# One block for a whole decoder-trunk kernel, with its instruction order from a detailed timing model

## The chip, the core and the metric

The kernel runs on one core of a Trainium2 chip. The core has five engines with an instruction queue each: TensorE (PE) for matmuls and transposes, VectorE (DVE), ScalarE (ACT), GpSimd (POOL) and SyncE (SP), which here issues the DMAs. Each engine takes its own instructions in the order in which the program holds them; engines wait for each other by semaphores. The metric is the time of one execution on the device in microseconds, as the median of several runs.

## What is computed

Two layers of a decoder trunk over 512 tokens of width 1024, in float32. Each layer adds three terms to h: a mixer of three kinds of attention heads, a gated feed-forward of width 2816, and a per-layer embedding.

```python
for i in range(DEPTH):                     # DEPTH = 2
    hn = rms_norm(h, norm_mix[i])
    proj = hn @ w_in[i]                    # split into q, k, v of all head groups, gates
    ...
    o_nsa = nsa_attention(...)             # 8 heads in 2 groups: compressed, selected, window keys
    o_fox = forgetting_attention(...)      # 4 heads, softmax with a learned decay
    o_sb = stick_breaking_attention(...)   # 4 heads
    o = rms_norm(jnp.concatenate([o_nsa, o_fox, o_sb], axis=2), head_norm)
    h = h + o.reshape(b, s, MIX_WIDTH) @ w_out[i]
    hn = rms_norm(h, norm_ffn[i])
    h = h + (jax.nn.silu(hn @ w_ffn_gate[i]) * (hn @ w_ffn_up[i])) @ w_ffn_down[i]
    gate = jax.nn.sigmoid(rms_norm(h, norm_ple[i]) @ w_ple_gate[i])
    h = h + (p[i] @ w_ple_proj[i]) * gate
return rms_norm(h, norm_final)
```

## The kernel before

**Arithmetic and tiles.** Every float32 operand of a large product is split into a high and a low part (`halves`, lines 197 to 201: ACT copies, DVE or POOL subtracts), and a product is three matmuls (`mm3`, lines 221 to 225: high by high, high by low, low by high). Tokens are four tiles of 128, the width is eight. Weights arrive in `wraw` (three buffers, by DMAs of SP) and leave as `whl` (five buffers). PSUM has eight banks in four groups: "d" (2), "s" (3), "t" (2), "o" (1).

**Stages.** `mixer` (line 456) normalizes h and transposes it (`norm_T`, line 372: tile `xnT` in PSUM, copied to `xT` by ACT, its low part by DVE at line 388), and runs the projections and four kinds of attention. `feed_forward` (line 1120) follows, then `layer_embedding` (line 1168), whose accumulators `ge` hold the embedding product and the gate product side by side; `pg` is the gate's sigmoid.

**The attention chains.** In `softmaxes` (line 773) an item takes scores on PE (`sc`, lines 787 and 789), a maximum on DVE (`mx`, line 792), exponentials on ACT (`p`, line 795), a reciprocal on DVE (`rc`), a scaling on POOL (line 800), transposes on PE (`pTp`, line 808), copies on ACT and DVE (`pT`, lines 813 and 814), and products with the values on PE (`no` for NSA, line 1004; `fo` for the forgetting heads, line 860). `cmp_maps` (line 917) opens each of the two NSA groups: compressed scores (`cs`, line 922), their copy (`cse`), transposes (`csT`, line 929), a softmax in `ce` on DVE and ACT (lines 934 to 949, its exponential at 939), and transposes back (`pcT`, line 952). A finished head goes through `head_out` and `norm_pair` (lines 606 to 641): `obot`, `pair`, `sq`, a matmul `ms`, two `rs`, `pair`, `on`. The tile `on` is what the output projection reads: partly in `accr` (streams W067, W167, W00123, W10123, woven into the attention), the last two k tiles with `wo4` and `wo5` in `acco` (lines 1107 to 1116), which also adds the result to h (`add_h`, line 1025).

**What sets the order.** Python traces the program in one sequence. `weave` (line 102) interleaves an attention stream with filler streams, as the string at line 1093 says:

```python
        spec = "KC;cmp:SQ,SK,SV;sb:NKS,NKW,GT,NQ0;nsa0:NQ1,FV,FQ;nsa1:FR,FK,W067;fox:W167,W00123,W10123;45"
```

The framework's scheduler then orders the instructions of each engine. It weighs their priority (the place in the trace, moved by `prio`, line 123, whose offsets OFE, OFN, OFP stand at line 100), the dependencies, the free buffers, and its own model of how long an operation takes. `tc.issue_after` adds a dependency by hand.

Of the kernel before, what the change touches and what calls it, by code (L numbers as in the profile page):

```python
# [42 lines left out]
def hybrid_trunk_kernel(  # L43
# [24 lines left out]
    upool = ctx.enter_context(tc.tile_pool(name="upool", bufs=1))  # L68
    small = ctx.enter_context(tc.tile_pool(name="small", bufs=6))
    ps = ctx.enter_context(tc.tile_pool(name="ps", bufs=1, space=PSUM))  # L70

    def bank(tag, shape=(P, 512), dt=F32, name=None):
        bufs = {"d": 2, "s": 3, "t": 2, "o": 1}[tag]
        return ps.tile(list(shape), dt, name=name or f"ps_{tag}", tag=tag, bufs=bufs)
# [1258 lines left out]
```

## Time and profile before

| | us |
|---|---|
| median of 3 runs | 1573.04 (1572.74 to 1576.78) |
| the profiled execution | 1575.22 |
| its span, first to last instruction | 1573.5 |
| PE busy in it | 1516.4 |
| DVE, ACT, POOL busy | 746.1, 733.1, 577.4 |
| mean granted clock of PE | 0.992 of full |

The profiled execution was one of the same program; what lies between its span and its time is start and end of the launch. A row of a timeline gives an instruction's start and its length in us, its engine, the line of the kernel, the operation and its tiles; in brackets stands how long the engine was idle before it, and what ended that. A row of a table of stretches gives the busy time of each engine in a part of the span, so that the idle time of an engine is the stretch less that. Matmuls overlap in the pipeline of PE: a row's length is longer than the distance to the next start. The clock column is the granted clock of PE, 1.00 being the higher of its two levels (2.4 GHz) and 0.50 the lower (1.2 GHz).

### The profile page before, as it was taken

Reading aid. Unit: us, or ns where it says so; the run is one execution under the profiler, and the core shown is the slowest. Engines: PE = TensorE matmul, PEld = TensorE weight load, DVE = VectorE, ACT = ScalarE, POOL = GpSimd, SP = SyncE. Lnnn points to the kernel's source line nnn. Section 1 sums busy time; section 2 is a strip of 40 time slices with the busy share of each in tenths; the row PEclk is TensorE's granted clock in tenths of the full one; section 3 lists DMA queues with packets and bytes.
Section 4 is the critical chain, followed back from the end, with each engine's and each line's share of the span. In section 5 each row is a group of like instructions: output and inputs, shape, how many; then the busy total and the mean of one; then the engine's idle time right before and its main releaser. Section 6 shows DMA issues by size and latency. Waiting matters only on the chain.

```text
span 1573.5 us, 23178 instructions
## 1 busy us (share of the span) xinstructions
PE 1516.4 (96%) x8626; PEld 1286.3 (82%) x8626; DVE 746.1 (47%) x1588; ACT 733.1 (47%) x1561; POOL 577.4 (37%) x636
## 2 busy tenths in 40 slices
PE   6999999999999999999999999999999999999997
PEld 6898877879888888888988988778788888888887
DVE  7777869763211111214386878796621111112153
ACT  5467667654333332323355767686433333323243
POOL 4323545453333333321233235465333333323223
PEclk9999999999999999999999999999999999999999
DMA  5411321122333323321224121212133323333221
GB/s 163 136 56 42 82 68 34 48 95 70 97 102 94 94 94 121 119 96 67 81 72 126 49 71 52 80 33 75 55 103 98 94 94 94 100 114 121 94 70 65
DMA packets 114449, 134.58 MB, mean 86 GB/s; under 512 B 6864, under 2 KB 91936, under 8 KB 114336
## 3 DMA queue, kind: packets, MB, share of 16 engines
q1 hardware_dynamic: 114336, 133.10, 27.5%
q8 instruction: 68, 1.11, 0.3%
q14 instruction: 45, 0.37, 0.1%
HBM read 122.59 MB, written 2.10 MB: 79 GB/s over the span
## 4 chain that ended last, share of the span: by engine, by line
PE 73%; DVE 9%; issue 7%; POOL 4%; ACT 4%; DMA 3%; SPq 0%; POOLq 0%; ACTq 0%; DVEq 0%
PE gu L223 10%; PE gu L224 10%; PE gu L222 10%; PE acc L222 6%; PE acc L223 6%; PE acc L224 6%; PE sc L787 2%; PE pTp L808 2%; PE no L1004 2%; PE accr L222 2%; POOL whl L201 2%; PE accr L223 2%; PE accr L224 2%; PE z L698 1%; DMA wraw<-in_w_ple_gate_dram 1%
## 5 line engine op out<-in xcount | busy, mean ns | idle before, releaser
L201 POOL TENSOR_TENSOR whl<-wraw,whl 128x512 fp32r<-128x512 f32 (+2 forms) x248 | 333.7, 1350 | 706.8 <-ACT whl L198 607.6
L198 ACT ACTIVATE whl<-wraw 128x512 fp32r<-128x512 f32 (+2 forms) x416 | 260.6, 631 | 483.0 <-PE gu L224 290.3
L201 DVE TENSOR_TENSOR whl<-wraw,whl 128x512 fp32r<-128x512 f32 x168 | 127.7, 761 | 496.8 <-ACT whl L198 496.1
L224 PE MATMUL gu<-xT,whl 128*128 128x512 f32 (+1 forms) x768 | 287.4, 374 | 0.0
L223 PE MATMUL gu<-xT,whl 128*128 128x512 f32 (+1 forms) x768 | 287.3, 374 | 0.0
L222 PE MATMUL gu<-xT,whl 128*128 128x512 f32 (+1 forms) x768 | 286.8, 373 | 0.0
L223 PEld LDWEIGHTS gu<-xT,whl 128*128 128x128 f32 x768 | 144.2, 188 | 27.5
L224 PEld LDWEIGHTS gu<-xT,whl 128*128 128x128 f32 x768 | 144.2, 188 | 27.4
L222 PEld LDWEIGHTS gu<-xT,whl 128*128 128x128 f32 x768 | 144.4, 188 | 27.1
L223 PE MATMUL acc<-whl,hid 128*128 128x512 f32 x352 | 139.7, 397 | 0.0
L222 PE MATMUL acc<-whl,hid 128*128 128x512 f32 x352 | 139.4, 396 | 0.0
L224 PE MATMUL acc<-whl,hid 128*128 128x512 f32 x352 | 138.8, 394 | 0.0
L800 POOL TENSOR_SCALAR p<-p,rc,gt 128x128 f32<-128x128 f32 (+3 forms) x128 | 79.2, 629 | 71.1 <-DVE rc L798 20.8
L795 ACT ACTIVATE p<-sc,mx 128x128 f32<-128x128 f32 (+3 forms) x160 | 83.9, 536 | 23.0 <-DVE mx L792 21.1
L814 DVE TENSOR_TENSOR pT<-pTp,pT 128x512 fp32r<-128x512 f32 (+2 forms) x120 | 70.6, 595 | 21.2 <-ACT pT L813 20.2
L813 ACT ACTIVATE pT<-pTp 128x512 fp32r<-128x512 f32 (+2 forms) x120 | 62.1, 527 | 38.6 <-PE pTp L808 37.3
L224 PEld LDWEIGHTS acc<-whl,hid 128*128 128x128 f32 x352 | 66.4, 189 | 15.3
L222 PEld LDWEIGHTS acc<-whl,hid 128*128 128x128 f32 x352 | 66.2, 188 | 15.1
L223 PEld LDWEIGHTS acc<-whl,hid 128*128 128x128 f32 x352 | 66.1, 188 | 15.3
L222 PE MATMUL acc<-whl,xT 128*128 128x256 f32 x256 | 74.0, 290 | 1.3 <-DVE rot_b L410 0.6
L792 DVE TENSOR_REDUCE mx<-sc 128x1 f32<-128x384 f32 (+4 forms) x120 | 70.2, 592 | 7.4 <-PE sc L789 7.2
L224 PE MATMUL acc<-whl,xT 128*128 128x256 f32 x256 | 73.3, 288 | 0.0
(298 smaller groups left out, 3320.7 us busy)
## 6 DMA issues: line engine op xcount, KB each, us to landing
wraw<-in_w_ffn_gate_dram SPq DMA_DIRECT2D x44, 512.0 KB, 3.6
wraw<-in_w_ffn_up_dram SPq DMA_DIRECT2D x44, 512.0 KB, 3.6
wraw<-in_w_ffn_down_dram SPq DMA_DIRECT2D x44, 512.0 KB, 3.6
wraw<-in_w_in_dram SPq DMA_DIRECT2D x36, 512.0 KB, 3.5
wraw<-in_w_out_dram SPq DMA_DIRECT2D x16, 512.0 KB, 3.7
wraw<-in_w_ple_gate_dram SPq DMA_DIRECT2D x16, 512.0 KB, 3.5
sw<-nq SPq DMA_DIRECT2D x32, 128.0 KB, 2.3
wraw<-in_w_in_dram SPq DMA_DIRECT2D x8, 280.0 KB, 2.9
```

Of the source, the lines that this page charges most:

```text
L198: se.activation(whl[:, 0], raw[:, lo:lo + n], AF.Copy)
L201: eng.tensor_tensor(whl[:, 1], raw[:, lo:lo + n], f(whl[:, 0]), op=ALU.subtract)
L222: i = te.matmul(acc, lhsT=lh, rhs=rh, start=start, stop=False, skip_group_check=True)
L223: te.matmul(acc, lhsT=lh, rhs=rl, start=False, stop=False, skip_group_check=True)
L224: te.matmul(acc, lhsT=ll, rhs=rh, start=False, stop=stop, skip_group_check=True)
L787: te.matmul(s[:, c:c + w], lhsT=lhsT, rhs=rhs, start=(j == 0), stop=False, skip_group_check=True)
L792: ve.tensor_reduce(mx, sv, axis=AX.X, op=ALU.max, negate=True)
L795: se.activation(e[:, u * n:(u + 1) * n], s[:, u * n:(u + 1) * n], AF.Exp, bias=mx[:, u:u + 1], accum_out=sm[:, u:u + 1])
L800: ge.tensor_scalar(e[:, u * n:(u + 1) * n], e[:, u * n:(u + 1) * n], rc[:, u:u + 1], gates[u] if gates else 1.0, op0=ALU.mult, op1=ALU.mult)
L808: te.transpose(pt[:, kt, :], e[:, kt * P:(kt + 1) * P], ident)
L813: se.activation(hi, src, AF.Copy)
L814: ve.tensor_tensor(lo, src, f(hi), op=ALU.subtract)
```

## The change

One line is added behind the pools. All that is traced after it, which is the whole computation, belongs to one block, and the order within this block is made with the scheduler's more detailed timing model. Nothing else is changed: the instructions of each engine, their operands, and the buffers are the same, and the numbers of lines and buffers rise by one.

```diff
--- before.py
+++ after.py
@@ -68,6 +68,7 @@
     upool = ctx.enter_context(tc.tile_pool(name="upool", bufs=1))
     small = ctx.enter_context(tc.tile_pool(name="small", bufs=6))
     ps = ctx.enter_context(tc.tile_pool(name="ps", bufs=1, space=PSUM))
+    ctx.enter_context(tc.block(schedule_with_timeline_sim=True))
 
     def bank(tag, shape=(P, 512), dt=F32, name=None):
         bufs = {"d": 2, "s": 3, "t": 2, "o": 1}[tag]
```

What moves is seen at three places. In the rows, buffers carry numbers where names alone would not tell them apart.

**ACT at the opening of the first NSA group, layer 0.** `cse` and `ce` belong to the compressed scores, `p` to the score sets of the group's first items (two heads by two branches of 128 columns make the first set, two branches of 256 each of the next two), `whl` to weights of the filler streams. Before:

```order
L926 ACTIVATE cse<-cs 128x512
L198 ACTIVATE whl<-wraw 128x520
L939 ACTIVATE ce<-ce 128x512
L795 ACTIVATE p,sm<-sc,mx 128x128 x4
L795 ACTIVATE p,sm<-sc,mx 128x256 x2
L198 ACTIVATE whl<-wraw 128x520
L795 ACTIVATE p,sm<-sc,mx 128x256 x2
L795 ACTIVATE p,sm<-sc,mx 128x384 x2
L954 ACTIVATE pc<-pcT 128x512
```

With the change:

```order
L927 ACTIVATE cse<-cs 128x512
L796 ACTIVATE p,sm<-sc,mx 128x128 x4
L796 ACTIVATE p,sm<-sc,mx 128x256 x4
L940 ACTIVATE ce<-ce 128x512
L796 ACTIVATE p,sm<-sc,mx 128x384 x3
L955 ACTIVATE pc<-pcT 128x512
```

The exponential of `ce` moved from ahead of the score sets to behind three of them, and the weight splits left the place. On PE, at the same place, 40 matmuls of the query projection stood between `csT` and `pcT`; now seven matmuls of another projection stand there, and more score matmuls.

**PE in the tail of the mixer, layer 0.** `pTp` and `fo` are those of the last forgetting head, `accr` with `on_2583` and `on_3415` is the output projection of earlier heads, `acco` the one of the last two k tiles. Before:

```order
L808 MATMUL pTp<-ident,p 128x128 x7
L860 MATMUL fo<-pT,fv 128x256 x4
L222 MATMUL accr<-whl,on_2583 128x512
L860 MATMUL fo<-pT,fv 128x256
L223 MATMUL accr<-whl,on_2583 128x512
L224 MATMUL accr<-whl,on_2583 128x512
L222 MATMUL accr<-whl,on_2583 128x512
L860 MATMUL fo<-pT,fv 128x256 x7
L223 MATMUL accr<-whl,on_2583 128x512
```

With the change (`on_4105` is the tile of the last two k tiles, `wo_4316` and `wo_4321` are `wo4` and `wo5`):

```order
L809 MATMUL pTp<-ident,p 128x128 x2
L861 MATMUL fo<-pT,fv 128x256 x7
L223 MATMUL acco<-wo_4316,on_4105 128x512
L224 MATMUL acco<-wo_4316,on_4105 128x512
L225 MATMUL acco<-wo_4316,on_4105 128x512
L809 MATMUL pTp<-ident,p 128x128 x7
L861 MATMUL fo<-pT,fv 128x256 x12
L635 MATMUL ms<-sq,ones_176 128x512
L223 MATMUL acco<-wo_4321,on_4105 128x512
L224 MATMUL acco<-wo_4321,on_4105 128x512
```

Before, two groups of twelve `accr` matmuls stood from the first `fo` of the last head to behind `ms`, and twelve `acco` with `wo4` behind them. With the change the `accr` and `acco` matmuls stand ahead of the seven `pTp`, and `fo`, `ms` and `acco` with `wo5` follow each other directly.

**PE in the per-layer embedding, layer 0.** `acc` is the end of the feed-forward, `ge` the embedding product, `xnT` the transposes of the normalized h. Before:

```order
L223 MATMUL acc_6592<-whl,hid 128x512
L380 MATMUL xnT<-ident,xn 128x128
L224 MATMUL acc_6592<-whl,hid 128x512
L380 MATMUL xnT<-ident,xn 128x128
L222 MATMUL acc_6592<-whl,hid 128x512
L380 MATMUL xnT<-ident,xn 128x128
```

With the change:

```order
L223 MATMUL ge<-we,pleT 128x256
L381 MATMUL xnT<-ident,xn 128x128 x4
L224 MATMUL ge<-we,pleT 128x256
L225 MATMUL ge<-we,pleT 128x256
L223 MATMUL ge<-we,pleT 128x256
```

Single transposes that alternated with single matmuls became four in a row, with several `ge` matmuls before the next four, and the feed-forward's last matmuls moved ahead of all of them.

## Rows read from the trace of the kernel before

**Rows 1.** The page, part 1: busy time of each engine, share, instructions.
```profile
PE 1516.4 (96%) x8626; PEld 1286.3 (82%) x8626; DVE 746.1 (47%) x1588; ACT 733.1 (47%) x1561; POOL 577.4 (37%) x636
```

**Rows 2.** Stretches of layer 0: window, length, busy per engine (instructions), PEclk, DMA.
```profile
156.00:183.00 27.00, 26.42 (x188) 22.49 (x188) 22.06 (x66) 17.20 (x47) 14.48 (x18) 1.00 0.38 99
227.00:250.00 23.00, 20.70 (x98) 15.49 (x97) 19.77 (x44) 12.73 (x36) 10.66 (x13) 0.93 0.15 46
250.00:290.00 40.00, 39.31 (x266) 32.47 (x265) 35.57 (x92) 31.80 (x81) 22.84 (x37) 1.00 0.16 41
328.00:346.00 18.00, 15.60 (x67) 12.13 (x66) 10.60 (x15) 6.65 (x12) 5.45 (x5) 0.91 0.33 103
346.00:365.00 19.00, 17.30 (x116) 14.91 (x116) 14.74 (x23) 9.77 (x24) 5.75 (x12) 1.00 0.01 3
715.00:740.00 25.00, 23.09 (x146) 19.58 (x145) 15.45 (x23) 11.28 (x22) 6.04 (x10) 1.00 0.24 84
765.00:802.00 37.00, 32.97 (x271) 31.89 (x270) 20.95 (x39) 15.12 (x36) 9.18 (x18) 1.00 0.20 58
```

**Rows 3.** The same columns for stretches of layer 1.
```profile
1104.00:1124.00 20.00, 18.22 (x84) 13.55 (x83) 12.58 (x17) 9.07 (x19) 9.01 (x10) 1.00 0.34 105
1490.00:1518.00 28.00, 26.12 (x172) 22.64 (x171) 16.29 (x25) 11.58 (x23) 6.02 (x10) 1.00 0.22 75
1518.00:1545.00 27.00, 25.27 (x212) 24.86 (x211) 13.26 (x18) 8.45 (x16) 12.63 (x8) 1.00 0.18 59
```

**Rows 4.** Waits of PE over the span: who for whom, us, times, longest.
```profile
PE sc L787 <- ACT p L795: 4.6, 2, 2.3
PE ge L222 <- DVE pg L1237: 3.4, 3, 1.6
PE cmp L523 <- DVE whl L201: 1.9, 2, 1.0
```

**Rows 5.** Timeline of PE at 327 us: start, length, engine, line, operation, tiles.
```profile
327.29 0.40 PE L222 MATMUL accr<-whl,on 128*128 128x512 f32 x1
327.52 0.39 PE L223 MATMUL accr<-whl,on 128*128 128x512 f32 x1
```

**Rows 6.** Timeline of PE and DVE, opening of the first NSA group.
```profile
159.52 0.66 PE L929 MATMUL csT<-ident,cse 128*128 128x128 f32 x4
...
168.39 0.60 PE L952 MATMUL pcT<-ident,ce 128*128 128x128 f32 x4
...
160.22 0.69 DVE L934 TENSOR_TENSOR ce<-csT,amask 128x512 f32<-128x512 f32 x1 [3.56 <-PE csT L929]
...
167.33 0.82 DVE L949 TENSOR_TENSOR ce<-ce,crc 128x512 f32<-128x512 f32 x1
```

**Rows 7.** The page, part 5: the score reductions of all softmaxes.
```profile
L792 DVE TENSOR_REDUCE mx<-sc 128x1 f32<-128x384 f32 (+4 forms) x120 | 70.2, 592 | 7.4 <-PE sc L789 7.2
```

**Rows 8.** Timelines of PE, DVE and ACT, layer 0's mixer tail.
```profile
330.48 1.12 PE L808 MATMUL pTp<-ident,p 128*128 128x128 f32 x4 [2.00 <-POOL p L800]
334.03 1.00 PE L860 MATMUL fo<-pT,fv 128*128 128x256 f32 x7
337.18 1.05 PE L634 MATMUL ms<-sq,ones 128*128 128x512 f32 x2
...
332.26 0.69 DVE L814 TENSOR_TENSOR pT<-pTp,pT 128x512 fp32r<-128x512 f32 x1 [1.65 <-ACT pT L813]
340.02 1.39 DVE L638 SCALAR_TENSOR_TENSOR pair<-pair,hgT,rs 128x512 f32<-128x512 f32 x1 [2.42 <-ACT rs L637]
...
341.44 0.63 ACT L640 ACTIVATE on<-pair 128x512 fp32r<-128x512 f32 x1 [0.42 <-DVE pair L638]
```

**Rows 9.** Stretches of 2 us behind three gaps of PE.
```profile
242.00:244.00 2.00, 2.00 (x6) 1.50 (x7) 2.00 (x11) 2.00 (x9) 0.80 (x2) 0.50 0.00 0
332.00:334.00 2.00, 2.00 (x8) 1.70 (x7) 0.69 (x1) 0.23 (x1) 0.00 (x0) 0.53 0.00 0
...
1020.00:1022.00 2.00, 1.65 (x9) 1.20 (x10) 2.00 (x9) 2.00 (x11) 0.38 (x1) 1.00 0.01 4
```

## The prediction

> **What bounds the kernel now.** I read the busy table first. TensorE (PE) is busy for 1516.4 of 1573.5 us, the other engines for less than half of the span each [rows 1]. So this is a PE-bound kernel, and a change that only reorders can do two things: take from, or add to, the 57.1 us in which PE stands idle. Next I cut the span into stages with the table of stretches; idle is the stretch less PE's busy time. In layer 0 it lies at the opening of the first NSA group (27.00 - 26.42 = 0.58 us), at that of the second (2.30), in the mixer's tail (2.40), in the norm behind it (1.70), and in the per-layer embedding with the handover to the next layer (1.91 and 4.03) [rows 2]. Layer 1 repeats layer 0, with 1.78 in the tail and 1.88 and 1.73 in the embedding [rows 3]. Last I read the waits of PE: score matmuls on the exponentials of ScalarE (ACT), embedding and compressor matmuls on VectorE (DVE) [rows 4].
>
> My currency is issue intervals, not durations: two neighbouring 128x512 matmuls start 0.23 us apart although each is shown as 0.39 or 0.40 long [rows 5]; 128x256 ones start 0.12 apart and 128x128 transposes 0.11, read the same way. All 8,604 matmuls at these intervals give 1460 us.
>
> The Trainium skill ("Trainium Kernel Development and Optimization", section Performance Expectations) calls matmul busy time a bad measure of how near a kernel is to its roof, because matmuls are pipelined; the trace agrees, as 0.39 against 0.23 us shows. What that would mean here is the first rival below.
>
> **The change part by part.** Instructions, tiles and buffers are the same on every engine; only their order changes, and in the feed-forward stages not even that. I compare, at each place, the PE work that the new order puts between two dependent PE instructions (the cover) with the chain on other engines that links them. What the cover lacks is new idle.
>
> *Opening of the first NSA group, both layers.* Compressed scores are transposed (csT), pass through a softmax on DVE and ACT (ce), and are transposed again (pcT). In the trace csT starts at 159.52 and pcT at 168.39, 8.87 us apart; DVE works from 160.22 to 168.15 without a gap, five score reductions (mx) among the chain's own operations [rows 6]. The old order has 40 projection matmuls there, so PE does not notice. The new order has seven; nearly all others come ahead of csT. Beside them stand 15 score matmuls (six of 512 columns at 0.23, eight of 384 at 0.17, one of 256) and eight small masks: 4.2 us, with csT 4.6. The chain meanwhile grows: DVE has nine mx inside it, four more at a mean 0.59 us [rows 7], 2.4; seven more small operations, about 0.6; and on ACT the exponential of ce moves behind those of three score sets, about 0.4 of it not hidden. 8.87 + 3.4 = 12.3. So idle is 12.3 - 4.6 = 7.7 at most, and 8.87 - 4.6 = 4.3 if the chain takes no longer than now. I take the middle, 6.0, less the 0.58 of now: **+5.4 per layer, +10.8** (bounds +3.7 to +7.1 each).
>
> *Opening of the second group.* PE waits here for ACT now (4.6 us in two times, one in each layer) [rows 4]; this goes, since two runs of 24 projection matmuls and 42 of the output projection are put before csT and pcT. But eight score sets of this group now stand among the last products of group 0: by the durations of their kinds ACT has 18.0 us to do there against 13.8 us of PE work, 4.2 short. Later, where this group's attention runs, 48 output-projection matmuls (11.1 us) are gone; ACT is busy for 31.80 of 40 us there and loses four weight splits with them (2.5 us), so 29.3 against 39.3 - 11.1 = 28.2, 1.1 short [rows 2]. 4.2 + 1.1 - 2.3 = 3.0, of which I give up 1.0 for the lead that ACT has when the stretch begins: **+2 per layer, +4** (0 to +5 each).
>
> *The mixer's tail.* The last head goes through pTp, pT, fo, head sum, square, ms, two rs, pair, on, acco. Now 24 matmuls of the output projection (5.5 us) and 12 with wo4 stand among these. The new order has them all earlier, and what is left is seven pTp, twelve fo, ms and then acco with wo5, one behind the other. From the rows [rows 8]: fo ends at 334.03 + 7 x 0.12 = 334.87 and ms starts at 337.18, so 2.3. From ms to the end of on it is 342.07 - 337.18 = 4.9, of which some 0.7 is the pair of 1.39 us, twice as long as DVE's operations of this size; 4.2 without it. From pTp to the end of the last pT it is 332.95 - 330.48 = 2.5, covered in part by pTp themselves and four fo; I take 1.0. The sum is 7.5, less 2.40 and 1.78 of now: **+5.1 and +5.7, +10.8** (+2.5 to +6.5 each). The present wait of 2.00 us on POOL is within the 2.40.
>
> *Clock.* A gap of about 2 us is followed by half speed or is not: after the wait for ACT in layer 0 the granted clock is 0.50, after that at 328 it is 0.53, after the same wait for ACT in layer 1 it is 1.00 [rows 9]. A fall lasts some 3.4 us and so costs 1.7. The fall in layer 0's second opening goes (-1.7), that in its tail stays, one in layer 1's tail comes (+1.7), where the gaps grow: **net 0**. The Trainium skill ("TensorE: Matmul & The Clock Gate", section HAM oscillation) has PE fall back to its lower clock again and again when it pauses between bursts of matmuls; what every new gap would cost by that is a rival below. The rows show both outcomes after gaps of this size.
>
> *Norm behind the mixer.* All accumulators close together, so eight additions to h, four pairs of xn and the xT copies queue on DVE, which is busy for 14.74 of 19.00 us there already [rows 2]: DVE's work up to the second pair of xT is 12.4 us against 7.5 of cover, up to 4.9 short where 1.70 is idle now. I take half of the difference: **+1.5 each, +3** (0 to +3.2 each).
>
> *What it saves.* In the embedding the transposes xnT come four in a row with 8 to 28 gate matmuls between, where single transposes alternate with single matmuls now; the products that wait for pg (3.4 us in three times) [rows 4] come 20 matmuls later. Of 1.91 + 4.03 I take 5.0, of 1.88 + 1.73 2.7. Compressor matmuls, placed after other work, save 1.6 of their 1.9 [rows 4]. PE has 28 fewer separate wait instructions, at some 0.04 us each: 1.0. Together **-10.3** (-5 to -13).
>
> **Sum.** 10.8 + 4 + 10.8 + 0 + 3 - 10.3 = +18.3 on the profiled execution (1575.22 us, span 1573.5), which lies 2.2 above the median of 1573.04. Added to the median: 1591 us, +1.2%. A difference under 0.3% (4.7 us) cannot be told from no change.
>
> **The rivals.**
> *Faster: stalls that busy time hides.* 1573.5 less 1460 is 113 us, and only 57.1 of it is idle; 56 us lie between matmuls that wait a little for a tile that is just late. A finer model of the engines' timing would put more work between just these pairs, all over the attention stretches. If a third of the 56 goes (-19) and the gaps above come to their lower ends (7.4 + 0 + 5 - 1.7 + 0 - 10.3 = +0.4), the time is 1554; if a seventh goes (-8), 1565. It decides from about 8 us on with all gaps at their lower ends, or from 27 with mine. For it: the matmuls of the embedding are spread in that manner. Against: in both openings and the tail the order does the opposite, it bunches the fillers.
> *No change.* The lower ends alone, +0.4: 1573. It would be so if ACT and DVE, rid of weight splits there, ran the same chains sooner.
> *Much slower: the clock falls behind every gap.* Three places in two layers at 1.7 each, +10: 1601, and 1607 with the first opening at +7.1 and the second at +4.
> *Nothing happens* is excluded, as the order does differ.
>
> **How the numbers follow.** Forecast with its neighbourhood (1578 to 1600) 0.59, the clock case 0.13, no change 0.15, faster 0.13. The time is that of the forecast, 1591. The range goes from 1569, which leaves out the faster case, to 1607, the upper figure of the clock case. Slower by over 0.3% is 0.59 + 0.13 = 0.72.
>
> **What would show it.** In the new profile: idle of 4 to 8 us on PE between csT and pcT of the first NSA group, ended by DVE; about 4 us between ms and acco with wo5, ended by ACT's on; 2 us ahead of ms, ended by ACT's sq; no embedding matmul waiting on pg; no 2.3 us wait of scores on ACT at the second opening; the feed-forward stages as long as now. I am wrong if the tail's idle stays under 4 us per layer, or if PE's whole idle time comes out below 57 us.

## The result, and the profile with the change

The changed kernel takes 1631.26 us (median of four executions, 1630.12 to 1632.41) against 1572.89 us of the kernel before on the same chip: a ratio of 1.0354, 95% interval 1.0336 to 1.0373. Timed once more beside the last experiments, it gave 1.0334 (1.0305 to 1.0364). So the change costs 3.4 to 3.5%, three times the +1.2% of the prediction and beyond the upper end of its range. The direction and most places were right, the size was not.

The profiled execution has a span of 1628.4 us, 54.9 more than before. Its page, part 1 (busy time, share, instructions of each engine):

```profile
PE 1539.5 (95%) x8626; PEld 1305.6 (80%) x8626; DVE 735.3 (45%) x1588; ACT 730.6 (45%) x1561; POOL 573.9 (35%) x636
```

Against [rows 1], the same 8626 matmuls show PE busy for 23.1 us more, and idle for 1628.4 - 1539.5 = 88.9 us where it was 57.1: **idle +31.8 us**. The other 23 us look like work and are not. The clock track of the trace has PE at half its clock for 89.7 us, against 24.5 before; in 74.4 us of them (20.1 before) it was issuing. At half clock 128x512 matmuls start 0.43 us apart (rows of the tail below, 371.05 and 371.48) against 0.23 at the full one [rows 5], so a little under half of such time is lost. Taken as half, it is 37.2 - 10.1 = **+27.1 us by the clock**; with 0.20 of 0.43 it is 25. This is an estimate. With the idle time it makes 57 to 59, so 2 to 4 us of small stalls between matmuls went.

A second profile of the changed kernel has 88.3 us of idle time and 76.6 us of issuing at half clock, so the sums hold from one execution to the next. A single stretch need not: half clock in layer 0's tail lasts 6.8 us here and 10.2 there.

**Where.** I compare both traces at equal progress of PE: every matmul weighs the distance to the next one that is usual for its kind in the kernel before (0.23 us for 512 columns), and the time between two points, less the weights between them, is what was lost there to idle time, clock and small stalls. The boundaries between stages are chosen; where one is shifted by some us, 1 to 2 us move between neighbours. Added time by stage, in us:

| stage | layer 0 | layer 1 | predicted for each |
|---|---|---|---|
| start of the mixer and compressor | -0.2 | +0.8 | -0.8 |
| stick-breaking heads | -4.5 | -4.7 | nothing |
| opening of the first NSA group | +10.2 | +10.5 | +5.4 |
| opening of the second | +4.9 | +6.5 | +2 |
| end of the second group, start of the forgetting heads | +12.2 | +11.4 | nothing of its own |
| tail of the mixer and norm behind it | +9.5 | +10.0 | +6.6, +7.2 |
| feed-forward | 0 | 0 | 0 |
| embedding | -6.5 | -5.3 | -5.0, -2.7 |

The table of stretches points the same way without weights (length, busy time per engine with instructions in brackets, granted clock, DMA). Layer 0 with the change: the opening of the first group, that of the second, the end of the second, the tail, the feed-forward, the embedding in two pieces, and its handover to the next layer:

```profile
168.00:181.00 13.00, 9.14 (x41) 5.86 (x40) 10.99 (x30) 5.65 (x23) 6.23 (x11) 0.71 0.06 14
...
226.00:250.00 24.00, 19.64 (x113) 15.87 (x114) 18.24 (x48) 15.33 (x43) 10.89 (x16) 0.93 0.01 2
...
318.00:332.00 14.00, 11.12 (x55) 8.18 (x55) 7.94 (x26) 8.36 (x24) 4.65 (x7) 0.76 0.07 16
...
360.00:376.00 16.00, 9.37 (x34) 6.52 (x32) 5.31 (x9) 5.87 (x11) 2.54 (x2) 0.79 0.26 80
...
396.00:757.00 361.00, 361.00 (x1642) 296.98 (x1641) 71.53 (x103) 114.62 (x195) 118.43 (x96) 1.00 0.31 99
757.00:772.00 15.00, 15.00 (x129) 14.90 (x127) 11.02 (x18) 7.79 (x15) 4.80 (x6) 1.00 0.30 106
772.00:796.00 24.00, 24.00 (x205) 24.00 (x204) 10.84 (x19) 9.76 (x17) 7.59 (x5) 1.00 0.39 116
796.00:828.00 32.00, 30.53 (x254) 29.84 (x254) 17.85 (x34) 14.71 (x36) 7.90 (x17) 1.00 0.16 47
```

The tail is idle for 16.00 - 9.37 = 6.63 us of 16 and has a mean clock of 0.79; before, it had 2.40 idle of 18 [rows 2]. The embedding and its handover, with 1.91 and 4.03 us of idle time before [rows 2], have none up to 796 us and 1.47 behind. In between, 361 us of feed-forward run without a gap.

The waits of PE (who for whom, total us, times, longest), from the second row of the view on:

```profile
PE ms L635 <- ACT sq L634: 8.6, 4, 2.2
PE xnT L381 <- DVE xT L389: 8.1, 5, 2.2
PE acco L223 <- ACT on L641: 5.8, 2, 2.9
PE pcT L953 <- DVE ce L950: 5.2, 2, 2.9
PE cmp L524 <- DVE whl L202: 5.2, 2, 2.6
PE accT L223 <- DVE fqk L591: 4.4, 2, 2.2
PE sc L788 <- ACT p L796: 4.2, 8, 1.4
PE accr L223 <- DVE h L1026: 3.3, 2, 1.6
```

Most stand two or four times, once or twice in each layer, and most are new or longer than before. Of [rows 4], the wait of `ge` for `pg` is gone, and so is the 2.3 us wait of `sc` for ACT at the second opening; but eight waits of `sc` for ACT of up to 1.4 us stand in its place, mostly at the first opening, 4.2 us together against 4.6. At the second opening PE now waits longest for DVE's `fqk` (2.20 us); the compressor's wait for `whl`, which I expected to go, grew from 1.9 to 5.2 us.

**The opening of the first group**, layer 0, by the timelines of PE, DVE and ACT (start, length, engine, line, operation, tiles; in brackets idle time and releaser):

```profile
180.60 1.12 PE L953 MATMUL pcT<-ident,ce 128*128 128x128 f32 x4 [2.26 <-DVE ce L950]
...
168.99 0.69 DVE L935 TENSOR_TENSOR ce<-csT,amask 128x512 f32<-128x512 f32 x1 [3.51 <-PE csT L930]
...
179.44 1.10 DVE L950 TENSOR_TENSOR ce<-ce,crc 128x512 f32<-128x512 f32 x1
...
173.64 0.24 ACT L796 ACTIVATION_READ_ACCUMULATOR p<-sc,mx 128x1 f32 x1
173.73 0.67 ACT L940 ACTIVATE ce<-ce 128x512 f32<-128x512 f32 x1
174.25 0.62 ACT L796 ACTIVATE p<-sc,mx 128x384 f32<-128x384 f32 x1
```

`csT` starts at 168.36, so csT to pcT takes 12.24 us (12.25 in layer 1) where it took 8.87 [rows 6]. DVE's part grew from 8 to 11.5 us, with reductions of scores between the chain's own steps, and the exponential of `ce` stands on ACT behind those of three score sets. That is the chain as predicted (12.3). The PE work between the two weighs 4.5 us at full clock (4.6 predicted), so 7.7 us are lost there: PE is idle for 1.36, 0.22 and 2.26 us, some 2.3 us go by the clock, and the rest lies in stalls too short to be listed. What was not predicted is the clock: it is at half from 173.3 to 187.0, for 13.65 us, and so also behind pcT.

**The tail**, PE in layer 0:

```profile
361.81 0.86 PE L861 MATMUL fo<-pT,fv 128*128 128x256 f32 x5 [1.48 <-DVE pair L614]
...
366.02 1.13 PE L635 MATMUL ms<-sq,ones 128*128 128x512 f32 x2 [2.06 <-ACT sq L634]
370.04 0.79 PE L223 MATMUL acco<-wo,on 128*128 128x512 f32 x1 [2.89 <-ACT on L641]
...
371.05 0.63 PE L223 MATMUL acco<-wo,on 128*128 128x512 f32 x1
371.48 0.63 PE L224 MATMUL acco<-wo,on 128*128 128x512 f32 x1
...
379.99 1.03 PE L381 MATMUL xnT<-ident,xn 128*128 128x128 f32 x8
```

The three with brackets are the gaps of the prediction, 6.4 us together in place of the 7.5 worked out from [rows 8]; the clock is at half from 367.9 to 374.7.

### The profile page after: what moved, and what is told of

It is laid out like the page before. It is cut to its first block, busy times and chain, and to the rows that moved or that the text cites. A ratio compares the mean times of both kernels' runs of the same rounds, so it can differ in the third digit from the quotient of the medians.

```text
span 1628.4 us, 23136 instructions
## 1 busy us (share of the span) xinstructions
PE 1539.5 (95%) x8626; PEld 1305.6 (80%) x8626; DVE 735.3 (45%) x1588; ACT 730.6 (45%) x1561; POOL 573.9 (35%) x636
## 5 line engine op out<-in xcount | busy, mean ns | idle before, releaser
L202 DVE TENSOR_TENSOR whl<-wraw,whl 128x512 fp32r<-128x512 f32 x168 | 123.6, 737 | 494.9 <-ACT whl L199 494.2
```

Source lines behind the costliest of these rows:

```text
L202: eng.tensor_tensor(whl[:, 1], raw[:, lo:lo + n], f(whl[:, 0]), op=ALU.subtract)
```

## The experiments

All ratios are to the kernel before, measured beside it on the same chip. Against the changed kernel (1.0334 to 1.0354) a ratio of 1.030 is thus 5 to 8 us less. The diffs are against the changed kernel where nothing else is said. Two readings compete: by the first, each gap is a local matter, and filling it gives its time back; by the second, the fillers (projection and output matmuls that wait for nobody) are too few for all chains of the attention, so that a filler put into one gap opens another.

### Is it the block or the timing model?

From the kernel before, with the scheduler's old model:

```diff
     ps = ctx.enter_context(tc.tile_pool(name="ps", bufs=1, space=PSUM))
+    ctx.enter_context(tc.block())
```

> The block alone, ordered by the timing model of before; its order on each engine is that of the kernel before, row for row. Expected by every theory: the time of the kernel before, ratio 1.000. Otherwise the block would cost something of its own.

Measured: 1576.09 us, ratio 0.9999 (0.9987 to 1.0012), with the waits of the kernel before in place:

```profile
PE sc L788 <- ACT p L796: 4.6, 2, 2.3
...
PE ge L223 <- DVE pg L1238: 3.5, 3, 1.6
```

The block costs nothing. All of the 3.4 to 3.5% comes with the order that the more detailed model makes.

### The order of the mixer alone

From the kernel before: the block with the detailed model is opened behind the first norm of each mixer and closed at its end, so that feed-forward and embedding keep the old order. The `issue_after` of the first compressor weights would reach across the block's edge and is left out.

```diff
         with tc.issue_after(last_act[0].ins):
             se.preload_act_table_set(LN_EXP)
+        held = ExitStack()
+        held.enter_context(tc.block(schedule_with_timeline_sim=True))
...
+        held.close()
         return add_h
```

> The detailed model for the mixer alone, from behind its norm to the last acco, in a block for each layer; norms, feed-forward and embedding are ordered by the model of before. By comparing the two traces at equal PE work, the changed kernel gains 6.5 and 5.3 us in the embeddings and loses 12.5 and 8.0 us at the norm behind the mixer. If both belong to the instructions ordered there, this kernel has neither: 1631 + 11.8 - 20.5 = 1622 us. If the norm's loss comes from the mixer's tail (accumulators that close together), it has that loss without the gain: 1643 us.

Measured: 1672.13 us, ratio 1.0614 (1.0591 to 1.0637), above both figures. Two of the waits:

```profile
PE xnT L380 <- DVE xn L368: 21.7, 10, 8.2
...
PE ge L222 <- DVE pg L1240: 3.4, 3, 1.6
```

The embedding's gain is gone, as the `pg` wait shows. The norm behind the mixer loses no less than in the changed kernel, though it has the old order here: its loss does not come from its own order. That it comes from how the tail ends is the reading left. But at equal progress the mixer loses more than in the changed kernel: 4.8 and 10.3 us at the entries, across which no work moves now, which neither figure counted, and some 9 in each layer at the end of the second group, for which I have no cause. So the run says nothing on the sum.

### The tail: wo4 put back

The `acco` products with `wo4` are held behind the last `fo`.

```diff
-                        mm3(accs[j], on_act(k, 0, tt), ...
+                        with tc.issue_after(latest["fo"].ins) if k == last[0] else ExitStack():
+                            mm3(accs[j], on_act(k, 0, tt), ...
```

> The changed kernel, but the first 15 acco matmuls with wo4 are made to follow the last fo matmul, in both layers, so that 3.5 us of work lie between fo and ms again. In the changed kernel PE idles 2.06 us there in each layer, then 2.89 us before acco with wo5, and the granted clock is at half for 6.8 us from the middle of this. Theory A (a gap costs its idle time and then half the time for which the clock falls): the 2.06 us go, the rest of the gap no longer brings so long a fall: 4 to 11 us under the changed kernel, 1620 to 1627 us. Theory B (a gap costs its idle time alone): 4.1 us less, 1627. Theory C (the loss isn't tied to these places, the fillers are only missed elsewhere): 1631.

Measured: 1623.02 us, ratio 1.0303 (1.0275 to 1.0330), span 1622.4.

```profile
PE acco L223 <- ACT on L641: 5.8, 2, 2.9
...
PE ms L635 <- ACT sq L634: 4.5, 2, 2.2
```

Fifteen matmuls, at 0.23 us each 3.5 us, stand between `fo` and `ms` now and take away the two 2.06 us waits in the tail (8.6 to 4.5 us; the two 2.2 us ones at the end of the second group stay), and the half clock there falls from 6.8 to 3.4 us. Layer 0 gains 5.6 us, layer 1 only 0.8. Up to the norm behind the tail both gain some 3 us (3.4 and 2.9). The difference arises in the norm: the half clock that the changed kernel has there in layer 0 (385.0 to 391.8 us) is missing in this trace, which gives 2.1 us more, and layer 1 has one here (1182.0 to 1188.8) that the changed kernel's trace does not have, which takes 2.1 us back. The 5 to 8 us of the ratio fit theory A; theory B's 4.1 is too near to be excluded.

### The clock in the tail

Eight matmuls go into the gap ahead of the tail's `ms` (into its own PSUM tile, which `ms` then overwrites) and eleven into a spare tile between `ms` and `acco`.

```diff
+            warm = pr == 5
+            if warm:
+                with tc.issue_after(latest["fo"].ins):
+                    for _ in range(8):
+                        te.matmul(pm, lhsT=negone, rhs=on_tiles[1][:, 0, 0, :], start=True, stop=True)
...
+                with tc.issue_after(latest["ms"].ins):
+                    for _ in range(11):
+                        te.matmul(idle, lhsT=negone, rhs=on_tiles[1][:, 0, 0, :], start=True, stop=True)
```

> The changed kernel with idle PE time filled by matmuls whose results nobody reads: 8 (128x512, 1.85 us) between the last fo and ms, 11 (2.5 us) between ms and acco with wo5, in both layers, where PE waits 2.06 and 2.89 us for ScalarE anyway. The waiting chain is as long as before, so only the clock can change. Theory A: the clock doesn't fall in the tail; half of 6.8 us in each layer, 6.8 less in all, about 1624.5 us. Theory B (the clock plays no part): 1631, or up to 1 us more.

Measured: 1627.31 us, ratio 1.0324 (1.0297 to 1.0350), 2 to 5 us less than the changed kernel; the intervals overlap, so the ratio alone does not settle it. Stretches of 2 us in the changed kernel, from 366 on (the clock is the third number from the end):

```profile
366.00:368.00 2.00, 1.13 (x2) 0.30 (x2) 0.00 (x0) 0.78 (x2) 0.00 (x0) 0.97 0.00 0
368.00:370.00 2.00, 0.00 (x0) 0.00 (x0) 0.75 (x1) 1.17 (x2) 0.00 (x0) 0.50 0.00 0
370.00:372.00 2.00, 1.97 (x5) 1.58 (x6) 0.00 (x0) 0.00 (x0) 1.27 (x1) 0.50 0.00 0
372.00:374.00 2.00, 2.00 (x6) 1.56 (x5) 0.00 (x0) 0.00 (x0) 0.00 (x0) 0.50 0.00 0
```

The same stretches with the dummies, then the two rows behind the gaps and the start of the next transposes:

```profile
366.00:368.00 2.00, 1.79 (x7) 1.10 (x7) 0.00 (x0) 0.78 (x2) 0.00 (x0) 1.00 0.01 4
368.00:370.00 2.00, 1.97 (x9) 1.27 (x7) 0.75 (x1) 1.15 (x3) 0.00 (x0) 1.00 0.00 0
370.00:372.00 2.00, 1.69 (x7) 1.43 (x8) 0.00 (x0) 0.25 (x1) 1.29 (x1) 1.00 0.00 0
372.00:374.00 2.00, 2.00 (x10) 1.44 (x9) 0.86 (x2) 0.14 (x1) 0.00 (x0) 1.00 0.00 0
```

```profile
366.29 1.12 PE L640 MATMUL ms<-sq,ones 128*128 128x512 f32 x2 [0.21 <-ACT sq L634]
370.31 0.50 PE L223 MATMUL acco<-wo,on 128*128 128x512 f32 x1 [0.33 <-ACT on L651]
...
378.10 1.03 PE L381 MATMUL xnT<-ident,xn 128*128 128x128 f32 x8
```

The dummies take no time from the chain (`acco` starts at 370.31 in place of 370.04, with the last `fo` 0.26 us later too) and the clock stays at 1.00. The stretch from 372 to 374 issues ten matmuls in place of six. So the fall does follow PE's idling. From the first `acco` to the first `xnT` the same matmuls take 7.79 us in place of 9.95 in layer 0 and 7.77 in place of 10.08 in layer 1: 2.2 and 2.3 us saved, for two episodes of 6.8 us in which PE issues for 4.7 and 5.1. From 367.9 to 370.0 the clock is at half while PE has nothing to issue, and that part costs nothing. So theory A's 6.8 was too much, and the account above counts only the time in which PE issues. Of the 4.5 us saved some 2 do not show in the total: layer 1's norm has half clock here from 1185.1 to 1191.9, which the changed kernel's trace does not have.

### The first opening: fillers put back

The projection NQ1, traced with the first group, has its last four k tiles held behind `csT`.

```diff
             if name == "NQ1":
-                return project(xact, w, allk, C_NQ + 256, 256, evac_nq(1))
+                return project(xact, w, allk, C_NQ + 256, 256, evac_nq(1),
+                               held=lambda k: tc.issue_after(latest["csT", 0].ins) if k >= 4 else ExitStack())
```

> The changed kernel, but the second half (k tiles 4 to 7) of the projection NQ1 is made to follow csT of the first NSA group, in both layers: 72 filler matmuls, about 8.6 us, now stand between csT and pcT instead of seven. The changed kernel idles there 1.26, 1.36 and 2.26 us in layer 0 and 0.68, 1.37 and 2.94 us in layer 1, and its clock is at half for 13.7 and 10.2 us behind that. Theory A (idle plus half of the time at half clock): 4.9 + 6.8 and 5.0 + 5.1 us go, 21.8 less, about 1610 us. Theory B (idle alone): 9.9 less at most, 1621. Theory C (missed elsewhere): within 3 us of 1631.

Measured: 1627.24 us, ratio 1.0331 (1.0304 to 1.0359): next to nothing. PE in layer 0:

```profile
153.54 1.12 PE L637 MATMUL ms<-sq,ones 128*128 128x512 f32 x2 [2.30 <-ACT sq L636]
...
156.85 2.12 PE L925 MATMUL cs<-nq,kcv 128*128 128x512 f32 x8 [0.88 <-DVE nq L439]
...
161.52 0.60 PE L932 MATMUL csT<-ident,cse 128*128 128x128 f32 x4
...
177.73 0.60 PE L955 MATMUL pcT<-ident,ce 128*128 128x128 f32 x4
```

No wait is left directly ahead of `pcT`; between `csT` and `pcT` PE still waits for 0.66 and 0.96 us in layer 0, and for 0.63 and 2.22 us in layer 1. Behind `csT` 10.4 us (8.3 in layer 1) are gained. But ahead of `csT`, from where the fillers were taken, `ms` now waits 2.30 us for ACT and `cs` 0.88 for DVE, and 7.7 (8.3) us are lost there. A gap moved. The 1610 of the first reading fell; the second was right.

### The first opening: the chain put first

At both openings DVE and ACT keep all their work, but the exponentials of the first eight score sets wait for that of `ce`, and the maxima from the sixth set on for the last operation on `ce`.

```diff
+                with tc.issue_after(latest["ce"].ins) if early_item and items.index(it) > 4 else ExitStack():
+                    ve.tensor_reduce(mx, sv, axis=AX.X, op=ALU.max, negate=True)
...
+                with tc.issue_after(latest["ce exp"].ins) if early_item else ExitStack():
```

> The changed kernel, but at the openings of both NSA groups the compressed softmax goes first again: ScalarE's exponentials of the first eight score sets follow the exponential of ce, and VectorE's score reductions from the sixth set on follow the last operation of ce. On VectorE five fewer reductions and six fewer small operations then stand inside the chain. Theory Q (the chain is late because these stand in its queues, as I priced with 3.4 us per opening): csT to pcT falls from 12.2 to under 9 us, PE is idle less and so spends less time at half clock: 4 to 10 us less than the changed kernel, 1621 to 1627. Theory L (VectorE and ScalarE have too much to do here whatever comes first, so the scores only wait in place of ce): within 2 us of 1631.

Measured: 1622.15 us, ratio 1.0295 (1.0271 to 1.0318). PE in layer 0:

```profile
171.41 0.60 PE L933 MATMUL csT<-ident,cse 128*128 128x128 f32 x4
178.06 0.69 PE L788 MATMUL sc<-nk,nq 128*128 128x384 f32 x1 [4.28 <-DVE csm L946]
180.82 1.06 PE L956 MATMUL pcT<-ident,ce 128*128 128x128 f32 x4
```

csT to pcT takes 9.41 us in place of 12.24, close to the 8.87 of before. So the other scores' work in the queues of DVE and ACT had lengthened the chain by 2.8 us. PE's wait did not go, it stands elsewhere (4.28 us on DVE, probably for score banks that the held reductions free later), but each layer gains some 3 us at this place (3.4 and 2.9), as the half clock there lasts 6.8 us in place of 13.65 and 10.2. At the second opening, where the edit acts too, nothing is gained on balance. The profiled execution is the slowest of the four (1628.1 us, the others 1619.4 to 1624.4), so its trace shows less gain than the ratio. The Trainium skill ("TensorE: Matmul & The Clock Gate", section Architectural detail, on queue depths) says that ACT and DVE are strict FIFOs; the trace agrees, as the `ce` exponential starts right behind the accumulator read of 173.64 in the changed kernel.

### The tail refilled, and both edits

The stream W10123 is traced behind the weave, its third token tile held behind the last `pTp`, the fourth behind the last `fo`, and `wo4` behind the last `ms`: the fillers of before, by hand.

```diff
-        spec = "KC;cmp:SQ,SK,SV;sb:NKS,NKW,GT,NQ0;nsa0:NQ1,FV,FQ;nsa1:FR,FK,W067;fox:W167,W00123,W10123;45"
+        spec = "KC;cmp:SQ,SK,SV;sb:NKS,NKW,GT,NQ0;nsa0:NQ1,FV,FQ;nsa1:FR,FK,W067;fox:W167,W00123;45"
...
+                                    held={2: "pTp", 3: "fo"} if name == "W10123" else {})
...
+        run(part("W10123"))
```

> The changed kernel, but the tail of the mixer has its fillers again, in both layers: 12 accr matmuls of W10123 follow the last pTp, 12 follow the last fo, and the acco matmuls with wo4 follow ms. They are taken from the stretch of the forgetting heads ahead of it. In the changed kernel PE idles in the tail for 1.5 + 2.1 + 2.9 us in layer 0 and 1.2 + 2.1 + 2.9 us in layer 1, and the clock is at half for 6.8 us in each. Theory P (the loss is bound to the place: the fillers were not needed where the new order puts them): 12.6 us of idle time less and about 2.5 us per layer of half clock less, 17 us less than the changed kernel, 1614 us. Theory S (the fillers are short everywhere, whoever takes them here opens a gap there, as with the first opening): 1624 to 1631.

Measured: 1617.95 us, ratio 1.0274 (1.0259 to 1.0289). Tail and norm gain 8.3 us in each layer, the stretch ahead of them gives back 2.7 and 4.1. The 9 to 13 us of the ratio lie between theory P (17) and theory S (0 to 7): the gaps of the tail close, and a smaller loss opens where the fillers were taken. With the edit of the first opening as well:

> The tail refilled as in the kernel before this one, and the compressed softmax first in its queues as in the experiment with ce. If the two places are independent, their gains add: that of the refilled tail (17 expected) and the 9 us measured for ce: 1605 us. If the gain of one is lost to the other: 1614.

Measured: 1612.07 us, ratio 1.0238 (1.0221 to 1.0255). The ratios of the two edits alone promise 16 to 22 us together; 15 to 18 came, so they act at separate places and nearly add up; the 1605 put down for that was missed because it took 17 us for the tail. PE's time issuing at half clock is 48.8 us here, against 74.4. It is the best of the versions with the detailed model, and still 2.4% slower than before.

### The end of the second group

To that, the 24 matmuls of W167 are held behind the last `no` of the second group, where `ms` waited 2.2 us for ACT.

```diff
+                                    dict.fromkeys(range(NT), "no") if name == "W167" else {})
```

> As t8 (tail refilled, ce first), and the 24 accr matmuls of W167 follow the last product of the second NSA group, in both layers; the changed kernel spends them between csT and pcT of that group. In t8 PE waits 2.2 us for the ms at the end of the group, ScalarE's and VectorE's head chain, with half clock for some 3.4 to 6.8 us, and 1.3 us ahead. Theory P (each chain end needs its own cover, and the opening of the group has enough): 2.2 us of idle time and about 2 us of half clock less per layer, 8 us less than t8: ratio 1.019. Theory S (fillers are short in the whole of the attention: 5.5 us of cover taken from the opening opens a gap of up to 5 us there): the ratio of t8, 1.024, or above.

Measured: 1612.90 us, ratio 1.0242 (1.0218 to 1.0266): no change against the version above. Waits of PE from 225 to 330 us, in that version:

```profile
PE ms L636 <- ACT sq L635: 2.2, 1, 2.2
...
PE sc L789 <- ACT p L800: 0.5, 2, 0.3
```

and with the fillers at the end of the group:

```profile
PE sc L789 <- ACT p L800: 2.9, 7, 1.2
```

The wait of `ms` is gone and 8.1 and 6.4 us are won at the end of the group; from 262 us on, where the fillers had stood, 9.2 and 7.0 are lost, with PE waiting for ACT's exponentials among others. The edit moves more than the 24: of the 60 `accr` matmuls between 249 and 275 us in the version above, 24 are left, so 12 others went along. As in the first opening, the gap moved.

### The embedding's gain, by hand

From the kernel before: its eight `xnT` held behind the feed-forward's last matmul, and the last embedding product 21 matmuls later, behind `pg`.

```diff
-        xact = norm_T()
+        xact = norm_T(latest["acc"])
...
+                if ci == 2 and n == 7:
+                    embed(3)
```

> The kernel before, with the embedding alone put into the order of the changed kernel by hand: the transposes xnT of the embedding's norm follow the last matmuls of the feed-forward (four in a row), and the products of the last quarter (those that waited for pg) come 21 matmuls later. By the comparison of the traces at equal PE work the changed kernel gains 6.5 and 5.3 us in these stretches. If this gain belongs to the order there: 5 to 11 us under the kernel before, ratio 0.993 to 0.997. If it hangs on the order of the stretches ahead: 1.000.

Measured: 1577.45 us, ratio 1.0004 (0.9991 to 1.0017). The waits:

```profile
PE xnT L381 <- DVE xT L389: 8.6, 9, 3.0
...
PE ge L222 <- DVE pg L1240: 1.2, 2, 0.6
```

The wait for `pg` falls from 3.4 us [rows 4] to 1.2, and that of `xnT` for `xT`, with single waits of up to 3.0 us, takes it back. So these two moves alone aren't what the detailed model gains here. Its spreading of the transposes over the `ge` matmuls is one reading left; that was not tried by itself.

## Why the prediction missed

**The clock was set at zero, and it is about half of the loss.** I took the change in the number of falls (one goes, one comes) at 1.7 us each, from the 3.4 us that the falls of [rows 9] lasted. Both parts failed. In the changed trace a stretch of half clock stands at 10 of the 13 waits of 2 us or more that PE has behind the first 60 us (the exceptions are the wait of 2.06 us in each tail, which has the fall at the longer wait next to it, and one of 2.16 us in layer 1's norm), and they last from 3.4 to 13.65 us, not 3.4. PE's time issuing at half clock grew by 54.3 us, so by the estimate above 25 to 27 us of the 54.9 are clock. The trace of the kernel before already had a longer fall behind shorter waits: the compressor's waits of 0.83 and 0.96 us in layer 1, then half clock from 832.2 to 839.0 us:

```profile
830.48 0.30 PE L523 MATMUL cmp<-bhl,whl 128*128 128x64 f32 x1 [0.96 <-DVE whl L201]
```

```profile
834.00:836.00 2.00, 2.00 (x6) 1.61 (x6) 1.48 (x6) 0.74 (x2) 0.05 (x1) 0.50 0.91 290
```

[rows 9] had shown both outcomes at gaps of this size; I read them as a coin with two sides that cancel, when I was forecasting three new gaps of 2 to 6 us in each layer, close together. The rival "the clock falls behind every gap" had the right mechanism, with too low a price for the same reason; its upper figure, 1607, adds up to 1609 by its own terms. The Trainium skill ("TensorE: Matmul & The Clock Gate", section HAM oscillation) describes this falling again and again between bursts; the trace agrees, and the dummies, which kept 1.00 where it was 0.50, show that in the tail the idling causes it.

**One place was missing.** From the second group's end to the forgetting heads 12.2 and 11.4 us were lost. The prediction has these products only as cover for the second opening. Waits there are `ms` for `sq` 2.23, `accr` for h 1.64 and `no` for `pair` 1.27 us in each layer; from 250 to 332 us PE is idle for 8.35 us in layer 0, and issues at half clock for 6.0. I had compared busy time of ACT with the stretch, which says whether an engine has enough to do, not whether a chain is covered; for the first opening and the tail I had followed chains, and there the gaps came out. The second opening was priced in the same way and cost 4.9 and 6.5 us in place of 2, with its longest wait on DVE's `fqk` and not on ACT's exponentials.

**Sizes that held.** csT to pcT: 12.3 predicted, 12.24 measured, though the idle time (1.36 + 0.22 + 2.26 = 3.8 us in layer 0) came out below the lower end of 4.3. The chain and its cover were right, and the 7.7 us between them were all lost; I took 6.0, the middle between this and a chain that does not grow, and with the clock behind pcT the place cost 10.2 us. Tail gross: 7.5 against 6.4. The norm: 1.5 against two waits of 2.18 and 1.61 us in layer 0, and their share of the clock. The embedding saved 11.8 in place of 7.7 us, but the two moves that the prediction named for it gave nothing by hand (1.0004), so its figure came near without its mechanism being shown. Feed-forward: unchanged.

**Signs that failed.** The compressor's wait for `whl` grew by 3.3 us in place of going. The stick-breaking heads gained 9.2 us in the two layers together, a part of the rival "stalls that busy time hides" that I had not put into the sum. The fillers that left the first opening stand ahead of `csT` now, in that stage, and when half a projection went back, 7.7 us were lost there.

**What this says of the cause.** The order of the detailed model appears to spend the fillers early: the stages that come first in the mixer, and the embedding, get faster, and the chains at the end of each attention stage stand bare. Fillers moved back to the opening (net 0 to 3 us of 10) or to the group's end (net 0) open the gap that they leave; in the tail, the last stage, moving them back gives a net 9 to 13 us, and putting the `ce` chain ahead of other work on DVE and ACT 6 to 9. By the measured ratios these two explain 15 to 18 us of the loss. The other 37 us are not traced to single moves: that they come from too little cover over the whole attention is what the two moved gaps suggest, and the old order was not restored stage by stage without the cost of a block's edge. Why the scheduler's detailed model prefers this order also stays open. No version with it beat the kernel before.

## What to carry over

When a reordering bunches the work that waits for nobody, follow each dependent chain through the whole stage and count its cover; an engine's busy share says nothing on that. Price a new idle gap of TensorE with the half-clock time behind it, not only with its length: here 31.8 us more idle time went with 25 to 27 us of clock. Before you refill a gap, look at where the filler comes from: in the middle of a stage it only moves the gap, and the gain is at the end of the chain of stages, or in shortening the chain itself.

## What the runs showed of the hardware

At the lower clock 128x512 matmuls started 0.43 us apart, at the higher one 0.23. The lower clock cost time only while TensorE issued: of the two tails' episodes of 6.8 us, PE issued in 4.7 and 5.1, and keeping the clock up saved 2.2 and 2.3 us. Matmuls that nobody reads, 8 and 11 of them in gaps of 2.06 and 2.89 us, kept the clock at 1.00 and did not delay the next needed matmul by more than 0.3 us. A fall can come without a wait of 2 us: in the kernel before, waits of 0.83 and 0.96 us stand ahead of half clock from 832.2 to 839.0 us. And the same pair of waits can be followed by the lower clock or not: behind the mixer, waits of 2.18 and 1.61 us in layer 0 have it from 385.0 to 391.8 us, waits of 2.16 and 1.77 us at the same place in layer 1 do not. The second profile of the changed kernel repeats this; with `wo4` put back it is the other way round. A comparison of two single traces can be off by some 2 us at this place for that reason.
